# A planned kernel whose five instruction queues are sorted a second time

## The chip, the cores and the metric

The kernel runs on one core of a Trainium2 chip. A core has five engines, each with its own instruction queue, worked off in the order in which the program wrote it: TensorE (PE, matrix multiplications, with weight loads shown as PEld), VectorE (DVE), ScalarE (ACT), GpSimd (POOL) and SyncE (SP, which here issues nearly all DMA transfers). An instruction that needs another engine's result waits at the head of its queue, and everything behind it on the same engine waits too. The metric is device time in microseconds (us), the median of several executions.

## What is computed

The reference is one layer of a streaming encoder for 1024 tokens of width 2048, in float32:

```python
u = einsum('bsd,de->bse', h, w_in)                  # one projection, 2048 -> 6752 columns
q, k, v, z_attn, q_idx, k_idx, w_idx, z_ssd, xbc, dt_raw = split(u)
# group A: sparse attention; an indexer of 16 heads scores the keys, each query keeps 256
score = einsum('bqhs,bqh->bqs', relu(q_idx . k_idx), w_idx)     # then top_k(score, 256)
o_attn = softmax_attention_over_kept_keys(q, k, v) * silu(z_attn)
# group B: Mamba-2 state-space mixer, causal conv, scan in chunks of 64, gated RMS norm
o_ssd = ssd_mixer(xbc, z_ssd, dt_raw, ...)
sub = einsum('bse,ed->bsd', concat(o_attn, o_ssd), w_out)       # 2048 -> 2048
h = layer_norm(2 ** 0.25 * h + sub)
```

## The kernel before

**Tiling.** The tokens are taken in two halves of 512. The projection runs over column tiles of 128 and over 16 slices of 128 input rows; each slice is one 128x128 weight and one 128x512 piece of the input. Every float32 operand is split into a high and a low part of type fp32r (`xh`, `xl` of the input, `wh`, `wl` of the weights, made by a copy on ACT and a subtraction on DVE or POOL), and three products, high times high, high times low and low times high, are added up in a PSUM bank (`pj`). Most of the projection and the output projection use block products in Strassen's manner, so sums of weight blocks (`wr<-wr,wr`, and `u<-u,u` with stores to `ts`) and sums of input blocks (`xf`) are formed on the way, and results of one product (P1, U2, U3) are stored and loaded again. PSUM has eight banks: four called `pj`, three `a` (index scores, attention scores, transposes, state-space pieces), one `o`.

**Stages.** The index heads and their scores come first (to about 300 us of the span), then top-k as a bisection in which ACT counts and DVE updates thresholds, while PE goes on with the projection; attention and the state-space chunks run as side tasks; the output projection fills the last part, with the layer norm of finished rows beside it. The functions that the later text names: `t_u` adds a loaded P1 to a PSUM bank (`u<-pj,u`), after which PE may go on adding into the same bank; `t_save` copies a bank out with ACT (`u<-pj`); `t_xst` loads and splits input slices; `t_wsum` forms the weight sums of the output projection, which are needed hundreds of microseconds later; `t_ssd` is one pair of state-space chunks, with two exponentials and eight activations of 128x128 on ACT; `t_oevac` adds an output bank to its running sum (`xh<-xh,pj`); `o_done` takes the statistics (BN_STATS), and `ln_apply` does the two layer-norm operations of a 128x512 block (`SCALAR_TENSOR_TENSOR ...,mv,...`).

**What sets the order.** The kernel has no order written by hand. While it is being built, a planner (`Flow`) keeps a clock for each engine from a table of costs (`Sim.cost`, L207) and rules for landing DMAs and for the port that DVE and POOL share. The projection's matmuls are the main stream (`emit_t`, `emit_o`). Everything else is a generator, a task, with a priority; `pump` goes through the tasks by priority, and a task whose needs are met by the planner's clocks (`ready`, L447, with 300 ns to spare for PE tasks) writes its next few instructions. An instruction is issued to the real engine at the moment when the planner places it (`Engine.call`, L320), so the queues of all five engines stand in the order of the planner's steps: a task's step is never taken back, and a group of instructions that one step writes stays together. Whether a subtraction goes to DVE or to POOL (`two`, `pick`) is settled at the same moment. All instructions carry the line of `Engine.call`, L321, in the profile; they are told apart by the tiles that they write and read.

Of the kernel before, what the change touches and what calls it, by code (L numbers as in the profile page):

```python
# [1 line left out]

# [94 lines left out]
class Port:  # L97
# [3 lines left out]
    def __init__(self):  # L101
        self.busy = []
# [34 lines left out]
class Sim:  # L137
# [69 lines left out]
    def cost(self, eng, op, outs, ins, kw, n):  # L207

        if eng == "PE":
            n = ins[1].free_size()  # L210
            if op == "transpose":
                return 111.0, 290.0
            if kind_of(ins[1]) == "float32":
                if outs[0].partition_size() <= 64:
                    return 111.0, 300.0
                return 2 * max(n / 2.4 + 4, 100.0) if n > 8 else 226.0, max(n / 2.4, 57.0) + 330
            return n / 2.4 + 14.5 if n > 128 else max(n / 2.4 + 4, 80.0), n / 2.4 + 176
        if eng == "V":
            m = max(x.free_size() for x in [*outs, *ins])
            scalar = any(x.free_size() == 1 for x in ins) and n > 1  # L220
            if op in ("max", "match_replace"):
                t = (155 if op == "max" else 261) + 1.042 * m
            elif op == "bn_stats":
                t = 160 + 1.042 * m
            elif op == "stream_shuffle":
                t = 180 + 1.042 * n
            elif op == "tensor_tensor_scan":
                t = 200 + 2.084 * n
            elif op in ("tensor_scalar", "tensor_copy"):
                t = 145 + (1.042 if in_psum(ins[0]) or in_psum(outs[0]) else 0.64) * n + 45 * scalar  # L230
# [28 lines left out]
    def run(self, eng, op, outs, ins, kw):  # L259

        if op == "dma_start":
            return self.dma(eng, outs[0], ins[0], kw)
        n = outs[0].free_size()
        at, notes = self.deps(outs, ins, eng)
        busy, took = self.cost(eng, op, outs, ins, kw, n)
        if eng == "A":
            kind = {AF.Silu: "silu", AF.Exp: "exp", AF.Ln: "ln"}.get(kw.get("func"))
            if kind and kind != self.table:
                self.table = kind
                self.clk["A"] += 1283  # L270
        start = want = max(self.clk[eng], at)
        if eng in "VG" and self.shares_port(eng, op, outs, ins, n):
            ns = busy if eng == "G" else max(busy - 20, 10)
            start, passed = self.port.take(eng, start, ns)
            if passed:
                later = start + ns - passed[0]
                for c in self.recent:
                    if c[1] >= passed[0]:
                        c[0] += later
                        c[1] += later  # L280
                for e in self.port.busy:
                    if e[2] == "V" and e[0] >= start:
                        e[0] += later
                        e[1] += later
                self.clk["V"] += later
            self.port.add(eng, want, start, ns)
        self.clk[eng] = start + busy
        cell = [start + took, start]
        if eng == "V":
            self.recent = self.recent[-24:] + [cell]  # L290
        self.note(notes, cell, eng)
        return cell

    def dma(self, eng, out, in_, kw):
# [13 lines left out]
        self.note(notes, cell, "D")  # L308
        return cell

class Engine:


    def __init__(self, flow, engine, name):
        self.flow, self.engine, self.name = flow, engine, name

    def __getattr__(self, op):
        f = getattr(self.engine, op)

        def call(*args, **kw):  # L320
            f(*args, **kw)  # L321
            is_ap = lambda x: hasattr(x, "tensor") and hasattr(x, "ap")
            outs = [x for x in args[:1] if is_ap(x)] + [kw[k] for k in ("out", "accum_out") if is_ap(kw.get(k))]
            ins = [x for x in args[1:] if is_ap(x)] + [x for k, x in kw.items() if is_ap(x) and k not in ("out", "accum_out")]
            if op == "tensor_tensor_reduce":
                outs.append(ins.pop())
            if op == "activation" and len(args) > 2:
                kw["func"] = args[2]
            self.flow.placed(self.flow.sim.run(self.name, op, outs, ins, kw))
        return call  # L330


class Engines:
    def __init__(self, flow, nc):
        for e, name in (("tensor", "PE"), ("vector", "V"), ("scalar", "A"), ("gpsimd", "G"), ("sync", "SP")):
            setattr(self, e, Engine(flow, getattr(nc, e), name))


class Event:
# [26 lines left out]
class Flow:  # L366
# [3 lines left out]
    SLACK = 2650.0  # L370
    MARGIN = 300.0

    def __init__(self, nc):
        self.sim = Sim()
        self.nc = Engines(self, nc)
        self.clk = self.sim.clk
        self.cells = []
        self.tasks = []
        self.pool = {}
        self.slots = {}  # L380
        self.where = {}
        self.n = 0
        self.idle = 0.0
        self.idles = []
        self.spare = 2
        self.resting = False
        self.pressed = False
        self.first = ("kv10", "kv11", "kv00", "kv01")
        self.spare_u = 9
        self.signals = []  # L390
# [201 lines left out]
class Layer:  # L592
    def __init__(self, ctx, tc, a):
        self.a = a
        fl = self.fl = Flow(tc.nc)
        nc = self.nc = fl.nc
        ctx.enter_context(tc.manual_schedule())
        pool = lambda name, **kw: ctx.enter_context(tc.tile_pool(name=name, **kw))
        self.cst = pool("cst", bufs=1)
        self.dram = pool("dram", bufs=1, space=bass.MemoryType.DRAM)  # L600
        for tag, n in (("xh", 16), ("xl", 16), ("xr", 2), ("wr", 6), ("wh", 3), ("wl", 3), ("u", NU), ("s4", N4), ("cv", 2), ("sm", 6)):
            fl.add_tag(tag, pool("p_" + tag, bufs=1), n)
        for tag, n in (("pj", 4), ("a", 3), ("o", 1)):
            fl.add_tag(tag, pool("ps_" + tag, bufs=1, space=bass.MemoryType.PSUM), n)
# [949 lines left out]
    seen = {}  # L1554
# [813 lines left out]
```

## Time and profile before

| | |
|---|---|
| time, median of 3 runs | 1654.28 us (1648.05 to 1657.73) |
| the profiled execution: its own time, and its span | 1656.14 us, 1654.3 us |
| PE busy | 1614.9 us, 98% of the span |
| PE weight loads | 1337.3 us, 81% |
| DVE, ACT, POOL busy | 1323.1, 1004.6, 204.2 us (80%, 61%, 12%) |
| mean granted clock of PE | 0.995 of full speed |
| DMA | 415.5 MB, 251 GB/s over the span |

A matmul is shown from its start to its modelled end, and the next one starts before that end, so a group's busy time counts such overlap once. "Idle before" and the views of waits name what the engine stood waiting for: `<-DVE u` is a DVE instruction that writes a tile called `u`. A number in a tile's name is left out in the profile and kept in the lists of the queues below.

### The profile page before, as it was taken

To read this page: it belongs to the slowest core of one execution; us is meant where nothing else is said; L and a number is where in the kernel's file an instruction comes from. 1 tells how busy PE (TensorE), PEld (TensorE's weight loads), DVE (VectorE), ACT (ScalarE), POOL (GpSimd) and SP (SyncE) were. 2 spreads that over 40 slices of the span, in tenths; PEclk is the share of its full clock that TensorE was granted. 3 is DMA by queue.
4 is the path that set the end of the run, shared out by engine and by line. 5 is a ranking of instruction groups with operands and counts; after the bars stand their busy time and mean duration, and the time that the engine had idled before them with its cause. 6 is when DMAs were issued, how large, how long until landed. Compare 5 with 4: busy or idle time off the path is not lost.

```text
span 1654.3 us, 23979 instructions
## 1 busy us (share of the span) xinstructions
PE 1614.9 (98%) x7996; PEld 1337.3 (81%) x7996; DVE 1323.1 (80%) x2429; ACT 1004.6 (61%) x1772; POOL 204.2 (12%) x220
## 2 busy tenths in 40 slices
PE   9999999999999999999999999999999999999987
PEld 7887677887787878787888888888888888888875
DVE  5889897997869966879667678886698788659998
ACT  4555555879886699783544465786866546433320
POOL 0000011000001001111112311333120100000210
PEclk9999999999999999999999999999999999999999
DMA  8287585689978977688566657466898999477654
GB/s 311 65 284 269 195 298 187 232 306 370 337 243 305 349 255 246 201 323 288 187 229 236 212 188 225 148 200 223 314 309 298 361 319 328 146 272 256 203 182 145
DMA packets 193467, 415.53 MB, mean 251 GB/s; under 512 B 19776, under 2 KB 56768, under 8 KB 193344
## 3 DMA queue, kind: packets, MB, share of 16 engines
q1 hardware_dynamic: 192912, 413.61, 72.6%
q8 instruction: 63, 1.03, 0.3%
q14 instruction: 60, 0.49, 0.1%
q10 hardware_dynamic: 432, 0.39, 0.1%
HBM read 309.46 MB, written 104.46 MB: 250 GB/s over the span
## 4 chain that ended last, share of the span: by engine, by line
PE 48%; DVE 13%; ACT 12%; DMA 7%; issue 4%; POOL 0%; SPq 0%; DVEq 0%; ACTq 0%; POOLq 0%
PE pj L321 37%; PE a L321 9%; ACT u L321 8%; DVE u L321 6%; DVE wl L321 3%; PE o L321 2%; ACT wh L321 2%; DMA wr<-wt 2%; DVE xl L321 2%; DVE xh L321 1%; DVE wr L321 1%; ACT s L321 1%; DVE s L321 1%; ACT L321 1%; DMA u<-xn 1%
## 5 line engine op out<-in xcount | busy, mean ns | idle before, releaser
L321 PE MATMUL pj<-xh,wh 128*128 128x512 f32 (+1 forms) x1496 | 583.0, 390 | 5.1 <-DVE u L321 3.1
L321 PE MATMUL pj<-xh,wl 128*128 128x512 f32 (+1 forms) x1496 | 571.8, 382 | 0.5 <-DVE wl L321 0.5
L321 PE MATMUL pj<-xl,wh 128*128 128x512 f32 (+1 forms) x1496 | 571.6, 382 | 0.1
L321 DVE TENSOR_TENSOR wl<-wr,wh 128x1024 fp32r<-128x1024 f32 (+2 forms) x235 | 281.5, 1200 | 148.1 <-ACT wh L321 147.4
L321 ACT ACTIVATE wh<-wr 128x1024 fp32r<-128x1024 f32 (+2 forms) x242 | 249.0, 1032 | 160.5 <-PE pj L321 117.7
L321 PEld LDWEIGHTS pj<-xh,wh 128*128 128x128 f32 x1496 | 282.8, 189 | 58.4 <-issue 3.7
L321 PEld LDWEIGHTS pj<-xh,wl 128*128 128x128 f32 x1496 | 282.3, 189 | 56.3 <-DVE wl L321 1.0
L321 PEld LDWEIGHTS pj<-xl,wh 128*128 128x128 f32 x1496 | 282.9, 189 | 50.0 <-DVE xl L321 0.5
L321 PE MATMUL a<-u,u 128*128 128x512 f32 (+3 forms) x744 | 177.5, 356 | 12.6 <-DVE s L321 5.3
L321 PEld LDWEIGHTS a<-u,u 128*128 128x128 f32 x744 | 120.5, 189 | 52.4 <-DVE s L321 20.4
L321 DVE TENSOR_TENSOR u<-u,u 128x512 f32<-128x512 f32 (+7 forms) x202 | 127.7, 642 | 21.4 <-DMA u<-wo 5.9
L321 ACT ACTIVATE u<-s,sm 128x896 bf16<-128x896 int16 (+7 forms) x132 | 129.5, 982 | 16.6 <-DVE sm L321 14.7
L321 PE MATMUL pj<-wh,xh 128*128 128x512 f32 x314 | 127.1, 405 | 5.4 <-DVE xh L321 4.7
L321 ACT ACTIVATE u<-u 128x512 f32<-128x512 f32 (+4 forms) x148 | 81.5, 558 | 71.5 <-DVE u L321 59.7
L321 PE MATMUL pj<-wh,xl 128*128 128x512 f32 x314 | 123.3, 393 | 0.0
L321 PE MATMUL pj<-wl,xh 128*128 128x512 f32 x314 | 123.0, 392 | 0.0
L321 ACT ACTIVATE a<-a 128x512 f32<-128x512 f32 (+3 forms) x160 | 76.5, 505 | 60.6 <-PE a L321 57.1
L321 DVE TENSOR_TENSOR u<-pj,u 128x512 f32<-128x512 f32 (+2 forms) x112 | 74.6, 667 | 43.1 <-PE pj L321 40.8
L321 ACT ACTIVATE u<-a 128x512 fp32r<-128x512 f32 (+4 forms) x118 | 53.0, 469 | 81.7 <-PE a L321 71.7
L321 DVE TENSOR_TENSOR wr<-wr,wr 128x1024 f32<-128x1024 f32 (+1 forms) x79 | 97.3, 1233 | 4.1 <-DMA wr<-wt 3.4
L321 POOL TENSOR_SCALAR s<-s,sm 128x640 f32<-128x640 f32 (+7 forms) x64 | 63.2, 1002 | 125.9 <-DVE sm L321 89.2
L321 DVE SCALAR_TENSOR_TENSOR s<-a,wsc,s 128x512 f32<-128x512 f32 (+3 forms) x120 | 73.2, 644 | 6.4 <-ACT a L321 4.3
(245 smaller groups left out, 2204.3 us busy)
## 6 DMA issues: line engine op xcount, KB each, us to landing
wr<-wt SPq DMA_DIRECT2D x187, 512.0 KB, 5.5
u<-u SPq DMA_DIRECT2D x110, 256.0 KB, 5.2
wr<-t SPq DMA_DIRECT2D x44, 512.0 KB, 5.6
u<-wo SPq DMA_DIRECT2D x64, 256.0 KB, 5.0
ts<-u SPq DMA_DIRECT2D x64, 256.0 KB, 4.1
wr<-ts SPq DMA_DIRECT2D x32, 512.0 KB, 5.1
s<-xt SPq DMA_DIRECT2D x25, 512.0 KB, 6.5
wr<-wo SPq DMA_DIRECT2D x23, 512.0 KB, 6.0
```

The lines of the kernel that those rows point to most:

```text
L321: f(*args, **kw)
```

## The change

The planner's order becomes a draft. `Engine.call` no longer issues; it records each instruction as an `Item` with its operands. The draft is planned in a program that is thrown away. Then `Order` takes the list of items:

- `link` finds for each item which others must come before it: those that write what it reads, that read or write what it overwrites, that held the buffer before. The buffers that the draft assigned stay as they are.
- `blocks` makes each matmul a block of its own; plain-float32 matmuls that follow each other stay together.
- `deadlines` gives every PE item the time at which PE would reach it without any pause, and walks back through the dependencies: an item on another engine is due in time for the earliest of its users, less its own duration, less 70 ns between engines; a DMA gets its transfer, its landing and 1500 ns more. What no PE item needs in the end is due at the end of time.
- `run` goes through the time with a clock for each engine. On DVE, ACT, POOL and SP the item with the earliest due time among those that are ready is taken (DVE and ACT at 1.03 of their cost, at most eight DMAs under way, a landing time that holds the 1500 ns too). On PE the first block in the draft's order that has been ready for 500 ns is taken, within the next 100 blocks.

`Program` writes the items into a fresh program in the order of their start. [...] Counted in the built programs, every engine has the same instructions as before but for these: 8 subtractions or sums move from POOL to DVE (6 more of 128x1024 and 5 more of 128x512 on DVE, 3 fewer of 128x256), there are 4 DMAs fewer of 1209, and ACT has 57 table loads instead of 55. The line of every instruction is now L611.

```diff
@@ Sim.cost
-                return 2 * max(n / 2.4 + 4, 100.0) if n > 8 else 226.0, max(n / 2.4, 57.0) + 330
+                return max(n / 0.6 + 8, 222.0) if n > 8 else 226.0, max(n / 1.2, 57.0) + 330
@@ class Engine
         def call(*args, **kw):
-            f(*args, **kw)
+            item = Item(self.name, op, args, dict(kw))
...
+            item.outs, item.ins, item.func = outs, ins, kw.get("func")
+            self.flow.items.append(item)
             self.flow.placed(self.flow.sim.run(self.name, op, outs, ins, kw))
@@ new
+class Order:
+    LATE = 1500.0
+    SLOW = 1.03
+    MARGIN = 500.0
+    WINDOW = 100
...
+    def gap(self, x, y):
+        if x.key == y.key:
+            return 0.0
+        return self.sim.LAT
...
+    def landing(self, x):
+        return (1350.0 if in_dram(x.outs[0]) else 1950.0) + self.LATE
+
+    def deadlines(self):
+        t = 0.0
+        for x in self.items:
+            x.due = 1e9
+            if x.key == "PE":
+                x.due = t
+                t += x.busy
+        for i in range(len(self.items) - 1, -1, -1):
+            x = self.items[i]
+            took = self.transfer(x) + self.landing(x) + x.busy if x.dma else x.took
+            for j in x.after:
+                y = self.items[j]
+                x.due = min(x.due, y.due - took - self.gap(x, y))
...
+    def next_block(self):
...
+        while n < len(self.block) and seen < self.WINDOW:
+            if not self.given[n]:
+                seen += 1
+                if self.wait[n] == 0:
+                    r = self.at[n] + self.MARGIN
+                    if r <= now:
+                        return n, now
+                    if at is None or r < at:
+                        best, at = n, r
+            n += 1
+        return best, at
...
+    def run(self):
...
+            while self.soon[q] and self.soon[q][0][0] <= t:
+                i = heapq.heappop(self.soon[q])[1]
+                heapq.heappush(self.now[q], (items[i].due, i))
+            i = heapq.heappop(self.now[q])[1]
+            x = items[i]
+            if x.dma:
+                lanes.pop(0)
+                data = max(data, t + 100.0) + self.transfer(x)
+                x.start, x.end = t, data + self.landing(x)
...
+                if x.port:
+                    t = self.free_port(x, t, busy if q == "G" else max(busy - 20, 10))
+                x.start, x.end = t, t + took
...
@@ kernel
     with tile.TileContext(nc) as tc, ExitStack() as ctx:
-        Layer(ctx, tc, a).run()
+        Program(ctx, tc, a, layer).emit(items)
```

The first place is the DVE queue at a `t_u` in the second third of the projection. `u_881<-pj_888` is the addition of P1 to a bank into which PE is to go on adding; the `xl` rows are `t_xst` splits of input slices that a later product uses. Before:

```order
L321 TENSOR_TENSOR wl_885_5160<-wr_855_4913,wh_884_5159 128x1024
L321 TENSOR_TENSOR xl_890_5175<-xr_870_5070,xh_889_5174 128x512
L321 TENSOR_TENSOR xl_892_5179<-xr_870_5070,xh_891_5178 128x512
L321 TENSOR_TENSOR wr_886_5163<-wr_886_5163,wr_887_5164 128x1024
L321 TENSOR_TENSOR xl_896_5196<-xr_871_5072,xh_895_5195 128x512
L321 TENSOR_TENSOR xl_898_5200<-xr_871_5072,xh_897_5199 128x512
L321 TENSOR_TENSOR xl_900_5210<-s4_872_5074,xh_899_5209 128x512
L321 TENSOR_TENSOR xl_902_5214<-s4_872_5074,xh_901_5213 128x512
L321 TENSOR_TENSOR xl_906_5228<-s4_873_5076,xh_905_5227 128x512
L321 TENSOR_TENSOR xl_908_5232<-s4_873_5076,xh_907_5231 128x512
L321 TENSOR_TENSOR u_881_5123<-pj_888_5167,u_881_5123 128x512
```

And in the changed program:

```order
L611 TENSOR_TENSOR wl_885_5034<-wr_855_4746,wh_884_5023 128x1024
L611 TENSOR_TENSOR xl_890_5042<-xr_870_4364,xh_889_5030 128x512
L611 TENSOR_TENSOR wr_886_4948<-wr_886_4948,wr_887_5000 128x1024
L611 TENSOR_TENSOR xl_892_5063<-xr_870_4364,xh_891_5044 128x512
L611 TENSOR_TENSOR xl_896_5071<-xr_871_4385,xh_895_5050 128x512
L611 TENSOR_TENSOR xl_898_5080<-xr_871_4385,xh_897_5056 128x512
L611 TENSOR_TENSOR u_881_4489<-pj_888_5021,u_881_4489 128x512
L611 TENSOR_TENSOR xl_900_5093<-s4_872_4282,xh_899_5060 128x512
L611 TENSOR_TENSOR wl_911_5100<-wr_864_4807,wh_910_5083 128x1024
L611 TENSOR_TENSOR xl_902_5109<-s4_872_4282,xh_901_5069 128x512
L611 TENSOR_TENSOR xl_906_5117<-s4_873_4293,xh_905_5077 128x512
L611 TENSOR_TENSOR xl_908_5124<-s4_873_4293,xh_907_5095 128x512
```

The addition has moved ahead of four splits, and a weight split stands between these.

The second place is the ACT queue at a `t_save`, the copy `u_1060<-pj_1058` that empties a bank for PE. `s4_974` and `u_979` are the chunk pair of a `t_ssd`, the rows with two outputs are counts of the top-k. Before:

```order
L321 ACTIVATE u_681_3735,sm_680_3734<-s4_109_745,sm_680_3734 128x896
L321 ACTIVATE u_681_3735,sm_680_3734<-s4_110_746,sm_680_3734 128x1024
L321 ACTIVATE u_1055_5985<-u_1055_5985 128x512
L321 ACT_TABLE_LOAD
L321 ACTIVATE u_979_5563<-s4_974_5558 64x512 x2
L321 ACTIVATE s4_974_5558<-s4_974_5558,ac0_241 128x128 x8
L321 ACTIVATE u_1060_6049<-pj_1058_6000 128x512
L321 ACTIVATE wh_1061_6053<-wr_1015_5755 128x1024
```

And in the changed program:

```order
L611 ACTIVATE cv_1054_5790<-pj_1039_5709 128x512
L611 ACTIVATE u_1077_5900<-u_1078_5824 128x512
L611 ACTIVATE u_1055_5905<-cv_1054_5790,cw_440 128x512
L611 ACTIVATE u_1048_5853<-u_1048_5853 128x512
L611 ACTIVATE wh_1061_5937<-wr_1015_5632 128x1024
L611 ACTIVATE u_1060_5947<-pj_1058_5881 128x512
L611 ACTIVATE u_1055_5905<-u_1055_5905 128x512
```

The two exponentials and eight activations of that chunk pair no longer stand ahead of the copy; they are some sixty rows earlier in the queue, the eight in groups of one, four and three.

The third place is the DVE queue in the output projection. The rows with `mv` are layer-norm operations of finished rows, which nothing but the stores to the output waits for; the rows that read `pj` empty banks that PE needs for the next product. Before:

```order
L321 SCALAR_TENSOR_TENSOR u_2896_15395<-u_2896_15395,mv10_15608,u_2906_15434 128x512
L321 SCALAR_TENSOR_TENSOR u_2896_15395<-u_2896_15395,mv10_15608,xh_2907_15435 128x512
L321 SCALAR_TENSOR_TENSOR u_2897_15397<-u_2897_15397,mv11_15611,u_2906_15434 128x512
L321 SCALAR_TENSOR_TENSOR u_2897_15397<-u_2897_15397,mv11_15611,xh_2907_15435 128x512
L321 TENSOR_TENSOR wl_2956_15722<-wr_2914_15473,wh_2955_15721 128x1024
L321 TENSOR_TENSOR s4_2958_15726<-wr_2923_15497,s4_2957_15725 128x1024
L321 TENSOR_TENSOR s4_2960_15730<-wr_2933_15541,s4_2959_15729 128x1024
L321 SCALAR_TENSOR_TENSOR u_2954_15692<-u_2954_15692,u_2734_14611 128x512
L321 TENSOR_TENSOR xh_2938_15589<-xh_2938_15589,pj_2937_15582 128x512
L321 BN_STATS u_2812_14966<-xh_2938_15589 128x6
L321 TENSOR_TENSOR xl_2939_15591<-xl_2939_15591,pj_2944_15601 128x512
```

And in the changed program:

```order
L611 SCALAR_TENSOR_TENSOR u_2894_15297<-u_2894_15297,mv10_15573,xh_2906_15246 128x512
L611 TENSOR_TENSOR u_2936_15332<-u_2936_15332,pj_2935_15561 128x512
L611 TENSOR_TENSOR wl_2954_15733<-wr_2919_15454,wh_2953_15712 128x1024
L611 TENSOR_TENSOR xh_2937_15481<-xh_2937_15481,pj_2942_15580 128x512
L611 TENSOR_SCALAR mv13_15721<-mv13_15721 128x1
L611 TENSOR_TENSOR u_2948_15577<-u_2948_15577,pj_2943_15594 128x512
L611 SCALAR_TENSOR_TENSOR u_2884_15239<-u_2884_15239,mv13_15721,xh_2896_15096 128x512
L611 SCALAR_TENSOR_TENSOR u_2895_15057<-u_2895_15057,mv11_15655,xh_2906_15246 128x512
L611 TENSOR_TENSOR xh_2952_15585<-xh_2952_15585,pj_2944_15605 128x512
```

The four operations that empty the banks (`pj_2935`, `pj_2942`, `pj_2943`, `pj_2944` here; `pj_2937` and its three neighbours before) now stand among the layer-norm operations instead of behind a run of them, and the statistics of these four blocks come later.

More of the change, by code (lines that the diff above doesn't have):

```diff
@@ L1 @@
 import bisect
+import heapq
 import numpy as np
@@ L309, in dma, with __init__, tile @@
         return cell
+class Item:
+    def __init__(self, eng, op, args, kw):
+        self.eng, self.op, self.args, self.kw = eng, op, args, kw
+        self.dma = op == "dma_start"
+class Pool:
+    def __init__(self, made, key, pool):
+        self.made, self.key, self.pool = made, key, pool
+    def tile(self, *args, **kw):
+        t = self.pool.tile(*args, **kw)
+        self.made[t.tensor.name] = self.key, args, kw
+        return t
 class Engine:
-    def __init__(self, flow, engine, name):
-        self.flow, self.engine, self.name = flow, engine, name
+    def __init__(self, flow, name):
+        self.flow, self.name = flow, name
     def __getattr__(self, op):
-        f = getattr(self.engine, op)
         def call(*args, **kw):
-            f(*args, **kw)
+            item = Item(self.name, op, args, dict(kw))
             is_ap = lambda x: hasattr(x, "tensor") and hasattr(x, "ap")
@@ new lines, with __init__, real, emit @@
+class Program:
+    def __init__(self, ctx, tc, a, layer):
+        self.nc, self.made = tc.nc, layer.made
+        ctx.enter_context(tc.manual_schedule())
+        self.pools = {name: ctx.enter_context(tc.tile_pool(name=name, **kw)) for name, kw in layer.pools.items()}
+        self.tiles = dict(a)
+    def real(self, x):
+        t = x.tensor
+        if t.name not in self.tiles:
+            key, args, kw = self.made[t.name]
+            self.tiles[t.name] = self.pools[key].tile(*args, **kw)
+        base = self.tiles[t.name]
+        if base.tensor.dtype != t.dtype:
+            base = base.bitcast(t.dtype)
+        return bass.AP(tensor=base.tensor, offset=x.offset, ap=x.ap)
+    def emit(self, items):
+        engines = {name: getattr(self.nc, e) for e, name in Engines.NAMES}
+        real = lambda v: self.real(v) if hasattr(v, "tensor") and hasattr(v, "ap") else v
+        for x in items:
+            getattr(engines[x.eng], x.op)(*[real(v) for v in x.args], **{k: real(v) for k, v in x.kw.items()})
@@ L371, with __init__ @@
     MARGIN = 300.0
-    def __init__(self, nc):
+    def __init__(self):
         self.sim = Sim()
-        self.nc = Engines(self, nc)
+        self.nc = Engines(self)
+        self.items = []
         self.clk = self.sim.clk
@@ L594, in __init__, with pool @@
         self.a = a
-        fl = self.fl = Flow(tc.nc)
-        nc = self.nc = fl.nc
+        fl = self.fl = Flow()
+        self.nc = fl.nc
         ctx.enter_context(tc.manual_schedule())
-        pool = lambda name, **kw: ctx.enter_context(tc.tile_pool(name=name, **kw))
+        self.made, self.pools = {}, {}
+        def pool(name, **kw):
+            self.pools[name] = kw
+            return Pool(self.made, name, ctx.enter_context(tc.tile_pool(name=name, **kw)))
         self.cst = pool("cst", bufs=1)
@@ L2363 @@
     a["out"] = nc.dram_tensor("out", (S, D), F, kind="ExternalOutput").ap()
+    draft = bacc.Bacc("TRN2", target_bir_lowering=False, num_devices=1, dynamic_dma_scratch_size=1024)
+    b = {k: draft.dram_tensor(k, v.shape, mybir.dt.from_np(v.dtype), kind="ExternalInput").ap() for k, v in arrays.items()}
+    b["out"] = draft.dram_tensor("out", (S, D), F, kind="ExternalOutput").ap()
+    with tile.TileContext(draft) as tc, ExitStack() as ctx:
+        layer = Layer(ctx, tc, b)
+        layer.run()
+        items = Order(layer.fl.sim, layer.fl.items).run()
     with tile.TileContext(nc) as tc, ExitStack() as ctx:
-        Layer(ctx, tc, a).run()
+        Program(ctx, tc, a, layer).emit(items)
     r = run_bass_kernel_spmd(nc, [arrays], core_ids=[0])
```

164 lines of the change are left out of this document (161 added, 3 removed).

## The prediction

> **What bounds the kernel now.** I read the page's busy times first, then the first and last PE rows of the timeline, then PE's waits.
>
> ```profile
> PE 1614.9 (98%) x7996; PEld 1337.3 (81%) x7996; DVE 1323.1 (80%) x2429; ACT 1004.6 (61%) x1772; POOL 204.2 (12%) x220
> 1.41 1.89 PE L321 MATMUL a<-s 128*128 128x512 bf16 x4 [1.41 <-POOL s L321]
> 1642.01 0.39 PE L321 MATMUL pj<-wr,xl 128*128 128x512 f32 x1
> PE a L321 <- DVE s L321: 5.3, 7, 2.5
> PE pj L321 <- DVE xh L321: 4.7, 1, 4.7
> PE pj L321 <- DVE u L321: 3.8, 5, 1.9
> PE a L321 <- DVE u L321: 3.2, 7, 0.7
> PE a L321 <- DVE sm L321: 2.1, 4, 0.8
> ...
> PE a L321 <- ACT u L321: 0.2, 1, 0.2
> ```
>
> PE is the bound: of the span's 1654.3 us only 39.4 are not PE's. Of these 1.4 lie ahead of the first matmul and 11.9 behind the last one, which ends at 1642.4. The rest, 26.1, is waiting inside the stream, and the view of waits (us in total, times, longest) lists it: twelve rows, first to last as shown, with 33 waits, most of them on DVE. The change issues the same matmuls, so it can only touch these waits and the two ends.
>
> A wait costs more than its idle time. Two matmuls in a running stream:
>
> ```profile
> 1571.76 0.39 PE L321 MATMUL a<-wh,xh 128*128 128x512 f32 x1
> 1571.99 0.39 PE L321 MATMUL a<-wl,xh 128*128 128x512 f32 x1
> ```
>
> They start 0.23 us apart but are shown for 0.39, so a stream that stops also loses 0.16 of overlap: 33 x 0.16 = 5.3 us. And three of the long waits are followed by a slow clock:
>
> ```profile
> 225.48:231.50 6.02, 6.02 (x27) 5.20 (x28) 5.96 (x9) 2.68 (x5) 0.73 (x1) 0.72 0.79 281
> 513.40:517.10 3.70, 3.69 (x9) 2.94 (x10) 3.70 (x4) 1.27 (x2) 0.51 (x1) 0.54 0.99 377
> 1577.94:1582.20 4.26, 4.26 (x12) 3.37 (x13) 4.19 (x6) 0.63 (x1) 0.00 (x0) 0.60 1.02 383
> ```
>
> The third number from the right is the granted clock. 6.02 x 0.28, 3.70 x 0.46 and 4.26 x 0.40 are each 1.7 us lost. All that stalls cost is so 26.1 + 5.3 + 5.1 = 36.5 us, and that, with the ends, is the most that any order could win.
>
> [...]
>
> **The change at four long waits.** The rows around each, in time: the culprit, the released instruction, PE.
>
> ```profile
> 510.17 2.49 DVE L321 TENSOR_TENSOR xl<-s,xh 128x512 fp32r<-128x512 f32 x4
> 512.58 0.68 DVE L321 TENSOR_TENSOR u<-pj,u 128x512 f32<-128x512 f32 x1
> 513.41 0.58 PE L321 MATMUL pj<-xh,wh 128*128 128x512 f32 x1 [1.86 <-DVE u L321]
> 594.73 1.28 ACT L321 ACT_TABLE_LOAD   x1
> 596.02 1.29 ACT L321 ACTIVATE u<-s 64x512 f32<-64x512 f32 x2
> 597.34 2.45 ACT L321 ACTIVATE s<-s,ac 128x128 f32<-128x128 f32 x8
> 600.32 0.51 PE L321 MATMUL pj<-xh,wh 128*128 128x512 f32 x1 [1.78 <-ACT u L321]
> 220.15 1.30 POOL L321 TENSOR_TENSOR u<-u,u 128x512 f32<-128x512 f32 x1 [7.17 <-DMA u<-wo]
> 221.47 0.69 DVE L321 TENSOR_TENSOR u<-u,u 128x512 f32<-128x512 f32 x1 [2.85 <-POOL u L321]
> 225.48 2.25 PE L321 MATMUL a<-u,u 128*128 128x512 f32 x6 [2.47 <-DVE s L321]
> 1566.64 2.26 DVE L321 SCALAR_TENSOR_TENSOR u<-u,mv,u 128x512 f32<-128x512 f32 x3
> 1572.19 4.50 DVE L321 TENSOR_TENSOR s<-wr,s 128x1024 fp32r<-128x1024 f32 x2
> 1577.21 0.68 DVE L321 TENSOR_TENSOR xh<-xh,pj 128x512 f32<-128x512 f32 x1
> 1577.94 0.50 PE L321 MATMUL pj<-wh,xh 128*128 128x512 f32 x1 [4.66 <-DVE xh L321]
> ```
>
> At 511 us the four splits, 2.49 us of DVE, stand ahead of the addition on which PE waits 1.86. The first pair of lists shows exactly these four rows behind it now. If nothing else is late, the whole wait goes: 1.86 + 0.16 + 1.7 = 3.7 us. What comes later instead are the splits, which serve a later product.
>
> At 598 us a table load, exponentials and activations, 5.0 us of ACT, stand ahead of a copy that frees a bank. The second pair shows them gone from there: 1.78 + 0.16 = 1.9 us. They ran far earlier in the new queue, where other copies could now stand behind them; there they come in groups of at most four, about 1.2 us, by 2.45 / 8 each.
>
> At 222 us DVE stands idle for 2.85 us at a weight sum for the output projection, which waits for a POOL sum, which waits for a load that landed late; behind it in the DVE queue are score updates that free PE's banks. Nothing needs this sum soon. The new pass waits with every user of a load for 1.5 us more than its landing, so this becomes rare: 2.47 + 0.16 + 1.7 = 4.3 us.
>
> At 1573 us layer-norm rows and two weight splits stand ahead of four additions that empty banks. The third pair shows them mixed now. This wait is worth 4.66 + 0.16 + 1.7 = 6.5 us, but only if DVE has room:
>
> ```profile
> 1480.00:1642.40 162.40, 157.00 (x682) 128.62 (x680) 155.37 (x227) 39.40 (x48) 18.75 (x12) 0.99 0.62 205
> 1571.05 1.22 DVE L321 TENSOR_TENSOR wl<-wr,wh 128x1024 fp32r<-128x1024 f32 x1
> ```
>
> From 1480 us to the last matmul DVE (third busy time) is busy 155.4 of 162.4, with 7.0 to spare. PE could finish 6.5 earlier only if nearly all of that were used. Between 0 (the stall comes back later) and 6.5 I take 4.5, nearer to the upper end, since part of the DVE time there was itself a loss: two splits took 4.50 us where one such split takes 1.22.
>
> Together 3.7 + 1.9 + 4.3 + 4.5 = 14.4 us.
>
> **The other 29 waits** are 26.1 - 10.8 = 15.3 us and 4.6 of overlap. Their new places I can't read from the old trace. Of the shown rows, the 7 on DVE `u`, 4 on `sm` and one on ACT `u` are 5.5 us, under half a microsecond each on average; the new pass takes a matmul only 0.5 us after its inputs are ready by its clocks, so such misses should mostly vanish. Bounds are 0 and all of their 5.5 + 12 x 0.16 = 7.4; I take 4.2, a little over half. The longer ones I leave as they are.
>
> **What the new order adds.** A queue is as fixed as before, so any misjudged time stops it again, at places that no trace shows yet. Lower bound 0; upper bound as much as the four places won, 14.4. The nearest rows are the many single waits of 1 us and less; I allow two of 1.1 + 0.16: 2.5 us. The 8 operations that leave POOL cost DVE about 6 x 1.23 + 5 x 0.70 - 3 x 0.41 = 9.7 us by these rows:
>
> ```profile
> L321 DVE TENSOR_TENSOR wl<-wr,wh 128x1024 fp32r<-128x1024 f32 x226 | 277.3, 1227 | 142.0 <-ACT wh L321 141.4
> L321 DVE TENSOR_TENSOR u<-u,u 128x512 f32<-128x512 f32 x125 | 87.2, 704 | 18.8 <-DMA u<-wo 5.9 <-DMA u<-zs 5.8 <-POOL u L321 2.8
> L321 DVE TENSOR_TENSOR u<-a,dt 128x256 f32<-128x256 f32 x30 | 12.5, 415 | 0.0
> L321 ACT ACT_TABLE_LOAD x55 | 70.6, 1283 | 3.1 <-issue 2.1
> ```
>
> I count them at nothing: DVE idles 331 us of the span under PE's stream; where it is full, as in the last part, each would cost what it takes. Two more table loads, 2.6 us, lie in ACT's 39% of idle time. The ends stay: the first matmuls wait for the same warm-up, and after the last one the new DVE queue holds the same twelve operations (addition, statistics, eight layer-norm halves), so I keep 1.4 and 11.9.
>
> **The sum.** 14.4 + 4.2 - 2.5 = 16.1 us. The profiled execution took 1656.1 us (span 1654.3), so 1640.0 against it; it lies 1.9 above the median of the runs, so about **1638 us** as a median.
>
> **Rivals.**
>
> *The waits only move.* The draft too placed every task by clocks, and its errors, not its rules, made the stalls; other errors now hit other places. For it: the model of costs and landings is nearly the same. Against it: at three of the four places the rows show a wrong priority, not a wrong time. Then 1654, give or take 7.
>
> *Loads stuck behind stores.* SP's queue is sorted without any reserve except the 1.5 us in a load's due time:
>
> ```profile
> SPq L321 <- DVE u L321: 259.4, 139, 13.6
> wr<-wt SPq DMA_DIRECT2D x187, 512.0 KB, 5.5
> ```
>
> A store that waits for DVE, 1.9 us each on average and up to 13.6, holds back every weight load behind it. It decides once such a wait exceeds the 1.5 us and PE's stock of weights is out. If one in seven of the 187 loads reached PE about 1 us late, 27 x (1.0 + 0.16) = 31 us would be added, and with half of my gain kept, 8, the time is 1654 - 8 + 31 = 1677. Against it: today's SP waits are as long, and no PE wait names a load.
>
> *The port of DVE and POOL.* POOL's operations were chosen where DVE's old queue left room; the new queues pair them anew. The 4.50 us for two splits, 2.1 over 2 x 1.22, ran beside a POOL split of 2.92 us. If 15 more such meetings hit DVE where PE hangs on it, 32 us of DVE time, half of it seen by PE: 1654 - 8 + 16 = 1662. [...]
>
> *It does not what it says*, because the draft's buffers bind the order: then little moves and the time stays at 1654. The three lists show that it moves.
>
> **How the numbers follow.** The forecast of a clear gain has 0.65, with its own range 1622 to 1647: the upper end of all bounds (6.5 and 7.4 taken whole, nothing added) is 1634, and the longer waits that I left would bring 1622. Waits that only move, or an order that hardly does, 0.22, within 1647 to 1661; stuck loads 0.07; the port 0.06, half of which stays below 1662. 0.5% is 8.3 us, about what can be told from no change here: faster (below 1646) 0.65, same 0.24, slower (above 1662.5) 0.11. The range for 8 in 10 is 1621 to 1660.
>
> **What would show it.** PE's waits in total fall from 26 to about 13 to 16 us, fewer than 33; no wait on `u<-pj` behind `xl` splits; no 4.7 us wait in the output projection, with DVE over 97% busy there; at most one spell of half clock; last matmul near 1627, tail near 12. I am wrong if the waits' total stays over 20, if PE's waits name DMA loads or `wl` (SP), or if the tail grows, because layer-norm work was put off past the last matmul.

## The result, and the profile after

The changed kernel took 1612.55 us (median; 1609.12 to 1615.60) against 1656.01 for the kernel before beside it: a ratio of 0.9746, with a 95% interval from 0.9706 to 0.9786. That is 43.5 us less, where 16.1 were predicted. The direction was right; the time is below the stated range, and the gain is more than the 36.5 us that I had called the most that stalls cost. The profiled execution has a span of 1612.2 us, 42.1 below the one before.

First the page of the changed kernel, PE's waits (us in total, times, longest) and its last matmul:

```profile
PE 1592.8 (99%) x7996; PEld 1338.9 (83%) x7996; DVE 1327.0 (82%) x2437; ACT 1005.9 (62%) x1774; POOL 213.3 (13%) x212
PE a L611 <- POOL sm L611: 2.9, 1, 2.9
PE a L611 <- DVE u L611: 2.1, 3, 0.8
PE a L611 <- POOL s L611: 1.4, 1, 1.4
...
1600.54 0.39 PE L611 MATMUL pj<-s,xl 128*128 128x512 f32 x1
```

Of about 26 us of waits on other engines in 33 places about 8 us are left, in 8 places (the 1.4 us ahead of the first matmul are in both lists), and none of the four long ones that the prediction took apart is among them. But PE's busy time fell too, by 22.1 us, with the same 7996 matmuls. A busy time that shrinks with the same work means that the old one held time in which PE did nothing, or worked at a lower clock. The view that shows it is that of the weight loads' waits (PEld). Before, and then after:

```profile
PEld a L321 <- DVE s L321: 20.6, 44, 2.7
PEld a L321 <- DVE u L321: 10.2, 20, 1.1
PEld a L321 <- DVE sm L321: 6.2, 13, 1.0
```

```profile
PEld a L611 <- POOL sm L611: 4.4, 3, 3.3
PEld a L611 <- DVE u L611: 3.4, 3, 1.2
...
PEld a L611 <- DVE s L611: 0.5, 2, 0.3
```

Before, 44 weight loads for `a` waited 20.6 us for DVE's score updates (`s`); PE's own list has only a few of these (5.3 us in 7), since a matmul is shown until its modelled end (0.39 us, with the next one 0.23 us after its start) and a short stop hides under it. The timeline of the kernel before, at the index scores:

```profile
186.29 2.26 DVE L321 SCALAR_TENSOR_TENSOR s<-a,wsc,s 128x512 f32<-128x512 f32 x3
187.27 2.07 PE L321 MATMUL a<-u,u 128*128 128x512 f32 x6
187.94 0.30 PEld L321 LDWEIGHTS a<-u,u 128*128 128x128 f32 x2 [0.48 <-DVE s L321]
188.60 0.30 PEld L321 LDWEIGHTS a<-u,u 128*128 128x128 f32 x2 [0.36 <-DVE s L321]
```

Six score matmuls stand together. Each pair needs a bank that DVE empties with one update of 0.75 us, while a pair at full speed takes 0.45 us; so the second and third pair start at DVE's pace, and PE's row still reads as busy for 2.07 us, where six matmuls 0.23 us apart would take 1.5. After:

```profile
180.10 0.62 PE L611 MATMUL a<-u,u 128*128 128x512 f32 x2
180.56 0.39 PE L611 MATMUL pj<-xh,wl 128*128 128x512 f32 x1
180.78 0.62 PE L611 MATMUL a<-u,u 128*128 128x512 f32 x2
181.24 0.39 PE L611 MATMUL pj<-xh,wh 128*128 128x512 f32 x1
181.47 0.62 PE L611 MATMUL a<-u,u 128*128 128x512 f32 x2
```

The pairs stand apart with projection matmuls between them. In the first 330 us the old order has 45 pairs that stand alone and 43 clumps of four to eight; the new one has 118 single pairs, 18 clumps of four and 2 of six. What that is worth is seen from the same stretch of both kernels (the columns are length; busy time and count of PE, PEld, DVE, ACT and POOL; granted clock; DMA share; GB/s):

```profile
0.00:300.00 300.00, 290.46 (x1406) 232.60 (x1407) 251.29 (x417) 170.89 (x302) 20.94 (x32) 0.99 0.65 227
```

```profile
0.00:300.00 300.00, 298.06 (x1535) 253.15 (x1536) 272.38 (x456) 183.32 (x320) 21.79 (x33) 1.00 0.73 256
```

PE gets through 129 matmuls more in the same 300 us, though it was already "97% busy" there.

To count all such losses I took, from the trace, the time from each matmul's start to the next one's, and subtracted the usual value for its tiles and shape (the median in the trace before). The sum of these excesses is what PE lost, seen or unseen. It fell from 67.3 to 25.6 us: intervals with a visible wait above 50 ns from 33.1 to 8.4, intervals in which the granted clock was halved (0.50 at 228 to 230, 514 to 516 and 1579 to 1581.5 us before, and at 1172.8 to 1174.9 us after) from 4.9 (three spells) to 1.6 (one), and all others, those shorter than usual taken off, from 29.3 to about 15.6. So of 41.7 us 24.7 were visible waits, 3.3 slow clock and 13.7 time lost where PE's list shows no wait. By stage, where a stage is a piece of PE's undisturbed time (index scores, projection with top-k, projection with attention, the rest of the side tasks, output projection; the first, 300 us of undisturbed work, took 322.8 us before), in us:

| kernel | to 300 | to 600 | to 1100 | to 1400 | output | tail | median |
|---|---|---|---|---|---|---|---|
| before | 22.8 | 9.7 | 17.0 | 10.2 | 7.7 | 11.9 | 1656.0 |
| changed | 0.7 | 2.3 | 7.4 | 15.4 | -0.2 | 11.2 | 1612.6 |
| PE kept | 19.8 | 3.4 | 17.3 | 14.2 | -0.2 | 11.2 | 1645.6 |
| only PE sorted | 18.3 | 11.7 | 17.6 | 19.7 | 6.4 | 14.9 | 1668.8 |
| SP kept | 31.7 | 3.9 | 7.8 | 18.3 | -0.2 | 13.9 | 1655.4 |
| DVE kept | 17.0 | 10.3 | 19.8 | 15.2 | -0.2 | 18.6 | 1656.4 |
| ACT kept | 5.8 | 29.1 | 11.5 | 19.6 | -0.2 | 11.2 | 1653.7 |
| no load reserve | 6.9 | 20.6 | 30.4 | 36.8 | 0.4 | 12.0 | 1683.4 |
| reserve 3000 ns | 0.6 | 0.3 | 5.5 | 9.8 | -0.2 | 12.3 | 1605.6 |

The lower rows are the experiments below. Half of the change's gain, 22.1 us, is in the first stage, 7.4 and 9.6 in the next two and 7.9 in the output projection; the stage before the output projection lost 5.2 us. That loss is largely one new wait, the longest in the changed kernel:

```profile
1168.87 2.82 POOL L611 TENSOR_TENSOR sm<-sm,mhalf 128x2 f32<-128x2 f32 x1 [19.31 <-DVE sm L611]
1171.74 0.71 PE L611 MATMUL a<-c,sm 128*128 128x128 f32 x4 [2.87 <-POOL sm L611]
1172.60:1176.60 4.00, 4.00 (x18) 3.40 (x18) 2.32 (x6) 3.95 (x11) 0.00 (x0) 0.57 0.97 378
```

A tiny POOL operation took 2.82 us, and 4.00 us at a granted clock of 0.57 follow, 1.7 us more: the same price of a slow spell as in the prediction.

### The profile page after: what moved, and what is told of

It reads as the page before. It is cut to its first block, busy times and chain, and to the rows that moved or that the text cites. A ratio compares the mean times of both kernels' runs of the same rounds, so it can differ in the third digit from the quotient of the medians.

```text
span 1612.2 us, 24012 instructions
## 1 busy us (share of the span) xinstructions
PE 1592.8 (99%) x7996; PEld 1338.9 (83%) x7996; DVE 1327.0 (82%) x2437; ACT 1005.9 (62%) x1774; POOL 213.3 (13%) x212
## 3 DMA queue, kind: packets, MB, share of 16 engines
q8 instruction: 63, 1.03, 0.3%
## 5 line engine op out<-in xcount | busy, mean ns | idle before, releaser
L611 PE MATMUL pj<-xh,wh 128*128 128x512 f32 (+1 forms) x1496 | 581.5, 389 | 0.0
L611 PE MATMUL pj<-xh,wl 128*128 128x512 f32 (+1 forms) x1496 | 571.2, 382 | 0.1
L611 PE MATMUL pj<-xl,wh 128*128 128x512 f32 (+1 forms) x1496 | 570.8, 382 | 0.0
L611 ACT ACTIVATE wh<-wr 128x1024 fp32r<-128x1024 f32 (+2 forms) x241 | 248.8, 1033 | 210.9 <-PE pj L611 185.9
L611 DVE TENSOR_TENSOR wl<-wr,wh 128x1024 fp32r<-128x1024 f32 (+2 forms) x236 | 283.4, 1201 | 63.8 <-ACT wh L611 61.3
L611 PEld LDWEIGHTS pj<-xh,wl 128*128 128x128 f32 x1496 | 281.5, 188 | 56.1 <-DVE wl L611 0.5
L611 PEld LDWEIGHTS pj<-xh,wh 128*128 128x128 f32 x1496 | 281.6, 188 | 50.8 <-issue 1.5
L611 PEld LDWEIGHTS pj<-xl,wh 128*128 128x128 f32 x1496 | 282.0, 189 | 49.0
L611 PE MATMUL a<-u,u 128*128 128x512 f32 (+3 forms) x742 | 172.6, 345 | 0.8 <-DVE u L611 0.5
L611 DVE TENSOR_TENSOR u<-u,u 128x512 f32<-128x512 f32 (+7 forms) x208 | 135.4, 661 | 15.0 <-ACT u L611 5.0
L611 PEld LDWEIGHTS a<-u,u 128*128 128x128 f32 x742 | 124.4, 190 | 19.8 <-DVE u L611 0.9
L611 ACT ACTIVATE u<-s,sm 128x768 bf16<-128x768 f32 (+7 forms) x132 | 129.0, 978 | 11.4 <-DVE sm L611 9.4
L611 PE MATMUL pj<-wh,xh 128*128 128x512 f32 x334 | 133.9, 401 | 0.0
L611 PE MATMUL pj<-wh,xl 128*128 128x512 f32 x334 | 130.5, 391 | 0.0
L611 PE MATMUL pj<-wl,xh 128*128 128x512 f32 x334 | 130.3, 390 | 0.0
L611 DVE TENSOR_TENSOR wr<-wr,wr 128x1024 f32<-128x1024 f32 (+1 forms) x83 | 102.9, 1241 | 24.1 <-DMA wr<-wt 23.3
L611 ACT ACTIVATE u<-u 128x512 f32<-128x512 f32 (+4 forms) x147 | 81.1, 558 | 57.2 <-DVE u L611 42.5
L611 ACT ACTIVATE a<-a 128x512 f32<-128x512 f32 (+3 forms) x160 | 78.0, 504 | 54.4 <-PE a L611 52.8
L611 DVE TENSOR_TENSOR u<-pj,u 128x512 f32<-128x512 f32 (+1 forms) x112 | 74.4, 665 | 21.7 <-PE pj L611 17.8
L611 POOL TENSOR_SCALAR s<-s,sm 128x640 f32<-128x640 f32 (+7 forms) x64 | 62.8, 992 | 193.8 <-DVE sm L611 153.8
L611 ACT ACTIVATE u<-a 128x512 fp32r<-128x512 f32 (+4 forms) x114 | 52.4, 477 | 44.1 <-PE a L611 40.5
```

Of the source, the lines that this page charges most:

```text
L611: getattr(engines[x.eng], x.op)(*[real(v) for v in x.args], **{k: real(v) for k, v in x.kw.items()})
```

## The experiments

Ratios are to the kernel before, in the runs beside each kernel, with their 95% intervals. Since every edit makes the second pass plan the whole program again, small differences may be chance of planning; I come back to that.

**The corrected cost alone.** The entry for a plain-float32 matmul in the planner's table of costs, which the change corrects too; that makes the draft a little different, and with it the choice between DVE and POOL. In the trace before, two such matmuls of 128x128 are four records 0.11 us apart (`a<-c,sm` at 687.3 us), where an fp32r one of 128x256 is a single record with the next 0.12 us after it. In the kernel before:

```diff
-                return 2 * max(n / 2.4 + 4, 100.0) if n > 8 else 226.0, max(n / 2.4, 57.0) + 330
+                return max(n / 0.6 + 8, 222.0) if n > 8 else 226.0, max(n / 1.2, 57.0) + 330
```

> The kernel before with the corrected cost of the plain-float32 matmul as its only edit; no second pass. Theory (the second pass makes the gain): the median stays within 1645 to 1662 us, and PE's weight loads still wait about 20 us in total (15 to 26) on DVE's score updates in the first 330 us. Rival (the corrected cost makes the planner's clocks right, and that is most of the gain): 1635 us or less, and those waits fall below 10 us.

Measured: 1661.88 us, ratio 1.0041 (1.0024 to 1.0058). The weight loads' wait on score updates is 19.7 us in 44 places, as before. The theory holds: the corrected cost by itself gains nothing, and costs a little.

**The second pass without it.** The same line put back in the changed kernel.

> The changed kernel with the old cost of the plain-float32 matmul, in the draft and in the second pass; all else as changed. Theory: 1609 to 1620 us. Rival (the second pass needs the right cost, since a plain-float32 group taken too short makes everything after it late): 1625 to 1645 us, with new waits of PE on ACT and DVE behind such groups.

Measured: 1605.73 us, ratio 0.9698 (0.9678 to 0.9717), so still faster than the theory said. The second pass is the whole gain, and it does not need the corrected cost.

**PE kept in the draft's order.**

```diff
-    WINDOW = 100
+    WINDOW = 1
```

> The changed kernel, but PE may look at only 1 block instead of 100, so PE keeps the draft's order; DVE, ACT, POOL and SP are sorted as in the change. Theory (the gain of 22 us in the first 300 us comes from PE's own new order, in which two thirds of the score matmuls no longer stand in clumps of four to eight that hang on DVE's score updates): the clumps stay, weight loads wait 12 to 22 us on DVE there, and the median is 1628 to 1645 us. Rival (the other queues' new order makes the gain; PE is merely released earlier): 1612 to 1620 us and under 6 us of such waits.

Measured: 1645.57 us, ratio 0.9937 (0.9916 to 0.9959), just above the upper end of the theory. The weight loads' waits to 330 us, and the group of score matmuls in the first 300 us:

```profile
PEld a L611 <- DVE s L611: 17.2, 24, 2.9
L611 PE MATMUL a<-u,u 128*128 128x512 f32 x178 | 53.6, 413 | 7.8 <-DVE s L611 7.4 <-DVE u L611 0.2
```

The clumps are back (45 single pairs, 43 clumps) and with them 17.2 of the 20.6 us. The first stage loses 19.8 us again, and the third 17.3. So three quarters of the gain hang on PE's own order; the four other queues by themselves give about 10 us.

**PE alone sorted.** DVE, ACT, POOL and SP are held to the draft's order:

```diff
+    KEEP = ('V', 'A', 'G', 'SP')
...
-            heapq.heappush(self.soon[x.eng], (x.ready, i))
+            if x.eng in self.KEEP:
+                self.free[i] = True
+            else:
+                heapq.heappush(self.soon[x.eng], (x.ready, i))
...
-            i = heapq.heappop(self.now[q])[1]
+            if q in self.KEEP:
+                i = self.queue[q][self.next[q]]
+                self.next[q] += 1
+            else:
+                i = heapq.heappop(self.now[q])[1]
```

> The changed kernel, but DVE, ACT, POOL and SP keep the draft's order strictly; only PE is sorted anew. Theory: the first 300 us keep most of their gain (under 7 us lost there, against 22.7 before and 0.8 in the changed kernel), while the waits behind splits and layer-norm rows stay (about 511, 598 and 1573 us of the old span, together 8 to 14 us), so 1620 to 1638 us. Rival (the other queues make the gain): 1645 us or more.

Measured: 1668.82 us, ratio 1.0084 (1.0055 to 1.0114). My theory fell. The clumps are halved (106 single pairs, 21 clumps), and yet the first stage loses 18.3 us: PE now waits for other things. (The line is L626 in the kernels with kept queues.)

```profile
PE pj L626 <- DVE wl L626: 7.7, 9, 1.5
PE pj L626 <- ACT u L626: 6.9, 3, 3.3
PE pj L626 <- DVE u L626: 4.7, 4, 2.4
PE pj L626 <- ACT wh L626: 4.6, 4, 3.5
```

It draws projection matmuls forward, and the splits `wh`, `wl` that these need stand where the old order had them. The time lies in the rival's range, but the run before shows that the other queues by themselves make no more than a quarter of the gain. PE's new order, which carries the rest, loses time unless the other queues move with it.

**One of the other queues kept.** The same edit with `KEEP` holding one queue: SP, DVE or ACT.

> The changed kernel, but SP issues its DMAs strictly in the draft's order; the four other queues are sorted as in the change. Theory (a DMA that waits at the head of SP's queue for a store's data holds back loads behind it, so SP's order must go with the others'): DVE's waits for loads rise above 40 us and the median is 1630 to 1680 us. Rival (loads are issued early enough in the draft's order too): 1608 to 1618 us.

> The changed kernel, but DVE keeps the draft's order strictly; PE, ACT, POOL and SP are sorted as in the change. The prediction put nearly all of the gain on DVE's order (three of its four places and most of the small waits). Theory (DVE's order carries at least half of the gain beside PE's): 1632 to 1665 us, with PE's waits on DVE above 15 us. Rival (DVE's old order does as well once PE and SP go another way): 1612 to 1625 us.

> The changed kernel, but ACT keeps the draft's order strictly; PE, DVE, POOL and SP are sorted as in the change. Theory (one queue left in the old order is enough to stop the others, since DVE's splits wait for ACT's copies): 1625 to 1665 us, with PE's waits on ACT back above 5 us. Rival (ACT, busy for 62% only, has the room to make up for it): 1610 to 1622 us.

Measured: SP 1655.38 us, ratio 0.9996 (0.9978 to 1.0014); DVE 1656.40, 1.0005 (0.9989 to 1.0021); ACT 1653.70, 0.9986 (0.9967 to 1.0004). All three times are those of the theories. Each of the three, kept by itself, takes the whole gain away. For SP the expected wait of DVE for weight loads did not come (14.8 us, less than the 23.3 in the changed kernel); the stop is one link earlier, at ACT, which waits 19.4 us for weight loads where the changed kernel has 2.1. SP's own waits that end between 262 and 273 us, ACT's row, and a piece of the timeline:

```profile
SPq L626 <- DVE s L626: 26.8, 2, 18.3
ACT wh L626 <- DMA wr<-wt: 19.4, 10, 6.9
284.31 1.06 ACT L626 ACTIVATE wh<-wr 128x1024 fp32r<-128x1024 f32 x1 [6.93 <-DMA wr<-wt]
285.40 1.23 DVE L626 TENSOR_TENSOR wl<-wr,wh 128x1024 fp32r<-128x1024 f32 x1 [3.31 <-ACT wh L626]
285.42 0.58 PE L626 MATMUL pj<-xh,wh 128*128 128x256 f32 x1 [2.64 <-ACT wh L626]
```

SP stands twice at a store whose sum DVE has not written yet, until 272.0 us. Then loads and stores go out in a crowd, and the weight load issued at 276.2 lands at 284.2. ACT has been idle for 6.9 us by then, DVE waits 3.3 for ACT's copy, PE 2.6. With DVE kept, PE waits for DVE's splits; with ACT kept, for ACT's copies out of the banks (one row of each):

```profile
PE pj L626 <- DVE wl L626: 13.1, 7, 4.3
```

```profile
PE pj L626 <- ACT u L626: 10.2, 3, 4.4
```

In these four kernels the pass knows the kept queue and plans the others around it, so its own clocks, which need no chip, tell whether the loss was planned or came as a surprise. The pass plans the end of PE's stream at 1581.7 us in the changed kernel, at 1614.9, 1616.7 and 1622.2 with DVE, SP or ACT kept, and at 1645.7 with all four kept. So 33 to 40 of the 41 to 44 us that one kept queue costs (64 planned, 56 measured for all four) are in the plan already. Most of the loss is not a wrong clock: one fixed queue fixes when everything that depends on it can be. POOL was not kept by itself.

**The due times.** Among the ready items of the four queues the one first in the draft is taken:

```diff
-                heapq.heappush(self.now[q], (items[i].due, i))
+                heapq.heappush(self.now[q], (float(i), i))
```

> The changed kernel, but on DVE, ACT, POOL and SP the item that comes first in the draft is taken among those that are ready, not the one with the earliest due time; PE as in the change. Theory (at three of the four long waits of the old kernel a ready but unhurried group stood ahead of an urgent one, so due times are needed): waits behind splits, a table load and layer-norm rows come back, the last part loses 4 us or more again, and the median is 1622 to 1645 us. Rival (it is enough that nothing unready stands at a queue's head): 1608 to 1618 us.

Measured: 1611.50 us, ratio 0.9736 (0.9708 to 0.9764), the same as with due times. The theory fell, and with it a reason of the prediction: it is enough that nothing stands at a queue's head that is not ready by the pass's clock. The output projection loses nothing without due times either (0.2 us less than undisturbed).

**PE's reserve and its look ahead.** `MARGIN = 0.0` for 500, and in another kernel `WINDOW = 12` for 100.

> The changed kernel, but PE may take a block at the moment at which its inputs are ready by the second pass's clocks, not 500 ns later. Theory (the clocks miss by some hundred nanoseconds on either side, and the reserve is what keeps such misses from PE): PE's waits rise from 6.7 us to 15 to 30 us, most of them under 0.6 us, and the median is 1620 to 1640 us. Rival (only the order counts, the reserve does nothing): 1608 to 1617 us.

> The changed kernel, but PE may look at 12 blocks ahead instead of 100. Theory (what frees PE from the score matmuls is a few projection matmuls put between two pairs, so a short look ahead does nearly all): clumps of four and more score matmuls fall from 43 of the old order to under 28, the first 300 us lose at most 6 us, and the median is 1611 to 1622 us. Rival (PE needs the deep look ahead): the first 300 us lose 12 us or more and the median is 1626 us or more.

Measured: 1616.99 us, ratio 0.9763 (0.9734 to 0.9792), and 1617.04, 0.9761 (0.9730 to 0.9793). The reserve's theory fell: without it PE waits 9.4 us in 11 intervals (6.7 in 10 with it), longest 2.3, no crowd of short ones. The look ahead of 12 blocks does nearly all: 109 single pairs, 24 clumps, and 3.0 us lost in the first stage.

**The reserve of loads.** `LATE = 0.0`, and in another kernel 3000.0, for 1500.0.

> The changed kernel without the 1500 ns that every DMA gets on top of its landing, in due times and in the second pass's clock. Theory (in the old kernel one long wait, at 222 us, came from a load that landed late; such cases are few): one to five new waits with a DMA behind them, 1612 to 1625 us. Rival (the reserve of the loads carries much of the gain): 1630 us or more, with PE's weight loads waiting for wl and wh after wr.

> The changed kernel with 3000 ns instead of 1500 ns on top of each DMA's landing. A 512 KB weight load took 4.9 us (median) from issue to landing in the changed kernel; the second pass's clock has 1.3 us of transfer, 1.95 us of landing and the reserve, so 3.2 us with 0, 4.7 with 1500 and 6.2 with 3000. Theory (what counts is that no instruction stands at a queue's head before its load is there): DVE's waits for weight loads fall from 23.3 us to under 10 us, and the median is 1600 to 1611 us. Rival (1500 is enough, more only takes room from other loads): 1612 to 1625 us, with SP waiting longer for free places.

Measured: 1683.41 us, ratio 1.0171 (1.0138 to 1.0205), and 1605.62, 0.9689 (0.9658 to 0.9719). Without the reserve the second pass is slower than no second pass. DVE's waits for weight loads with 0, 1500 and 3000 ns:

```profile
DVE wr L611 <- DMA wr<-wt: 68.4, 32, 5.6
```

```profile
DVE wr L611 <- DMA wr<-wt: 23.3, 17, 3.1
```

```profile
DVE wr L611 <- DMA wr<-wt: 9.5, 8, 2.5
PE a L611 <- POOL s L611: 1.4, 1, 1.4
```

With 3000 ns the second row is PE's whole list of waits: one, at the very start. Without a reserve, PE's list grows to 52.8 us in twelve rows. All but 0.3 us of it names DVE, ACT or POOL and none a DMA; the first three:

```profile
PE a L611 <- POOL sm L611: 10.8, 5, 4.1
PE a L611 <- DVE u L611: 10.7, 6, 3.1
PE a L611 <- DVE sm L611: 7.9, 6, 3.5
```

One such wait in the timeline of that kernel:

```profile
771.93 1.23 DVE L611 TENSOR_TENSOR wr<-wr,wr 128x1024 f32<-128x1024 f32 x1 [4.85 <-DMA wr<-wt]
773.07 0.68 DVE L611 CUSTOM_DVE_ANT_0 s<-a,u 128x512 f32<-128x512 f32 x1
773.82 0.79 PE L611 MATMUL a<-u,u 128*128 128x512 f32 x1 [3.48 <-DVE sm L611]
```

A late load parks DVE at a sum of weight blocks, and the operations behind it, which free PE's bank, come late. Here the clock of the pass is wrong: it plans the end of PE's stream at 1580.5 us, a little earlier than in the changed kernel, and the kernel takes 70.9 us longer. By start-to-start times 49.7 us of that are visible waits and 17.2 are spells of a slow clock, of which the changed kernel has one (mean granted clock 0.985, and 0.997 in the changed kernel); so late loads are paid twice. The median from issue to landing of a weight load is 4.9 us in the changed kernel; the pass's model gives 3.2 us without, 4.7 with 1500, 6.2 with 3000. So what is called a reserve is mostly the missing part of a landing. The 1500 ns stand in the due times as well as in the pass's clock; as due times made no difference in the run above, the clock is the likelier place, but no run parts the two.

**Where the rest lies.** The old cost in the draft and the corrected one in the second pass; and the old cost in both with 3000 ns:

> The changed kernel with the draft planned by the old cost of the plain-float32 matmul and the second pass by the corrected one. With the old cost in both, 1605.7 us were measured, with the corrected one in both 1612.6. Theory (the draft makes the difference: with the corrected cost it gives 8 operations more to DVE and places its tiles otherwise): 1603 to 1608 us. Rival (the cost in the second pass makes it): 1610 to 1616 us.

> The two single edits that gave about 1605.7 us each, in one kernel: the second pass with the old cost of the plain-float32 matmul, and 3000 ns on top of each landing. With the 3000 ns PE had one wait left (1.4 us, at the very start), so by the theory that only waits are to be won little is left: 1602 to 1606 us. Rival (the two gains add up): 1596 to 1601 us.

Measured: 1608.43 us, ratio 0.9705 (0.9667 to 0.9743), between the two theories; and 1607.60, 0.9719 (0.9702 to 0.9736), a little above what the theory said. The two single gains do not add up: nothing of the waits is left to be won. Why 1605.7 became 1612.6 with the corrected cost is open. Eight variants of the full pass lie between 1605.6 and 1617.0 us, and each plans everything anew, so a difference of some 7 us between two of them can't be put down to its edit from one such pair. The fastest kernels, at 1605.6 and 1605.7 us, beat both kernels of the case.

## Why the prediction was right and wrong

**What bounds it.** Right: PE, with the same 7996 matmuls, 1.4 us ahead of the first and 11.2 behind the last (11.9 before).

**The ceiling of 36.5 us. This is the step that failed.** "All that stalls cost" was read from PE's idle time and its list of 33 waits. PE lost 67.3 us by start-to-start times, and 29.3 of these stood neither in a visible wait nor in a slow spell. I put that part at nothing, and 13.7 us of the gain came from it. I had written that a stopped stream loses 0.16 us of overlap, and did not draw the conclusion: a stop shorter than that overlap shows no wait at all. The weight loads' list had it: 20.6 us in 44 places. The three slow spells were counted rightly.

**"The other 29 waits", 4.2 us. The second step that failed, a mis-sized term.** Visible waits and slow spells together gave 28.0 us, not 16.1. The four places were worth 16.4 in full by my own prices, so the rest came from the other waits. These were 15.3 us with the 1.4 at the start, which I had taken off once already, so 13.9. In the changed kernel at most 3.6 are left of them, beside the 1.4 and the new wait of 2.9. Some 10 us of idle time went where I had taken 4.2 with overlap. I counted only twelve waits, on `u` and `sm`, and left out six short ones on the score updates (DVE `s`). The first stage alone gave 22.1 us, of which the long wait at 222 us, on my own working, is 4.3. I looked at DVE's and ACT's lists at four places and never at how PE's new list mixes scores and projection, though the change lets PE look 100 blocks ahead. The run with PE kept shows what that is worth: 19.1 of the 22.1 us come back. My range, with its lower end at 1621, had the same two faults, and a slip in its sum: with 6.5 and 7.4 taken whole and nothing added it reaches 1630, not 1634.

**The four places, 14.4 us.** Right in size, wrong in the reason. All four waits are gone. The output projection went from 7.7 us lost to none; I took 4.5 for its long wait, and the stage won more than the full 6.5. DVE did have the room: from 1440 to 1601 us it is busy for 150.7 of 161 us, not the 97% that I named:

```profile
1440.00:1601.00 161.00, 160.92 (x710) 132.95 (x709) 150.67 (x227) 40.83 (x49) 11.53 (x9) 1.00 0.57 181
```

The reason that I gave, a wrong priority that due times mend, fell: without due times the same is won. A likely reason, which no run shows by itself, is that the old planner issued whole groups in one step; issued one by one when ready, the unhurried rows come apart without a rule for it.

**What the new order adds, 2.5 us.** Too low. The stage to 1400 us lost 5.2 us more than before, with a new wait of 2.87 us and its slow spell of 1.7.

**The rivals.** *Stuck loads*, priced at 1677 us, did not come in the changed kernel, but its mechanism is real: with SP kept, where a store holds SP until 272 us and a weight load behind it comes late, all of the gain goes. Without the 1500 ns the loads are not stuck but planned too early, and 1683.4 us were measured. I had given the reserve one wait at 222 us; of the numbers tried it is the most sensitive. I was also wrong on how late loads would show: PE's waits do not name them. *The port*, for which the planner has a rule: only the 2.82 us of the POOL operation at 1169 us, where its kind takes 1.0 us on average, looks like it; DVE ran two sums (1.28 us) and a split (1.22 us) meanwhile. Whether a shared port was the cause no run shows. *The waits only move*: that is what the runs with SP, DVE or ACT kept do (1653.7 to 1656.4 us), not the change.

**The slow spells.** Here again a wait of 2.87 us was followed by a slow spell, as waits of 4.66, 2.47 and 1.86 us were before. After the wait of 1.78 us the granted clock was 1.00 (600.3 to 606 us). How long a wait must be for a spell to follow, no run was made to show.

## What to carry to other kernels

Read the waits of the weight loads beside those of the matmuls, and compare start-to-start times with the undisturbed interval: an engine shown as 97% busy lost here 22.8 us on 300 us of undisturbed work, about two fifths of it (8.9 us) in stops that its own list of waits does not show. When in-order queues are re-planned, re-plan all of them together, with the real landing time of loads in the clock. PE's queue left in the old order cost three quarters of the gain here, that of SP, DVE or ACT all of it, and loads taken 1.5 us too early more than all of it. Where a model of the clocks is rough, the rule "issue only what is ready by then" did the work, and due times added nothing that could be measured.

## What the runs showed that was not expected

- With all waits gone (3000 ns) the span is 1603.6 us, and PE still loses 16.0 us by start-to-start times: about as much as some 150 single projection matmuls take together by being 60 to 200 ns longer than usual, without any wait shown. The kernel before has 166 of them and the changed one 148; what makes them is open.
- Loads and stores were issued in another order at nearly the same volume (415.5 and 414.5 MB), yet a weight load landed in 4.9 us instead of 5.5 (medians). Why is open.
